# One decoder layer on one core: modulation sums moved off the spatial gating unit, the mLSTM's first ends four ticks later, the last k tiles taken result by result

## The chip, the cores and the metric

The kernel runs on one core of a Trainium2 chip. The metric is the device time of one execution in microseconds (us). Engines are named as the profile names them: PE is the matrix engine, PEld its weight load, DVE the vector engine, ACT the scalar engine, POOL is GpSimd, and SP issues all DMAs of this kernel. "L1045" is line 1045 of the kernel before.

## The reference, cut to what matters

One layer is applied to x (2048 tokens x 1024 channels, float32). From the vector c come six modulation vectors; two parallel branches and an attention are computed from one projection:

```python
mod = silu(c) @ w_ada + b_ada            # 6 x 1024: shift, scale, gate, twice
h = rms_norm(x, g_mix) * (1 + sc1) + sh1
p = h @ w_in                             # q,k,v of attention; q,k,v,o and gates of mLSTM; u,v of the spatial unit
y = concat(forgetting_attention(...), sigmoid(o_m) * rms_norm(mlstm_chunkwise(...)),
           spatial_gating(gelu(u_s), gelu(v_s)))
x = x + gt1 * (y @ w_out)
h = rms_norm(x, g_ffn) * (1 + sc2) + sh2
x = x + gt2 * conv_ffn(h, w_up, w_conv, b_conv, w_down)
```

The mLSTM ends with h / max(|den|, exp(-m)) and an RMS norm over the 64 channels of each head. Every large product is computed from float32 split in two parts, with three matmuls for one (`mm3`, L53 to L56: high*high, high*low, low*high).

## The kernel before, in words

**Stages.** The kernel runs the projection of x into p (about the first 710 us of the profile), attention, the output projection, the up-projection with convolution, and the down-projection. Only the projection and the very end of the down-projection are touched.

**Steps and blocks.** The projection goes over two halves of the tokens (1024 each) and, in each half, over seven column blocks of w_in. That makes 14 steps, numbered n = 0 to 13: in the first half 0 km (mLSTM's k with the gates, 272 columns), 1 qo (mLSTM's q and o, 512), 2 vm (mLSTM's v, 256), 3 sgu (the spatial unit's u and v, 512), 4 k, 5 q, 6 v of the attention (512 each); in the second half 7 to 13 in the same order. A step has eight blocks, i = 0 to 7. A block is 24 matmuls into one PSUM tile `acc` (three buffers in turn) and then its consumer: `use_km`, `do_qo`, `use_vm`, `use_sgu`, `use_qk`, `use_v`.

**Ticks.** Everything else is threaded between the matmuls by hand, by `tick` (L627). `products` (L601) calls it at the end of each block and, where the block is 512 columns wide, also in its middle, after the fourth of eight k. This text writes "4-5m" for the middle tick of block 5 of step 4, and "4-5e" for its end. One tick does three things in this order: `due()` runs what was put off by `after(n, f)`, n ticks ago; then, in a middle tick, one segment of `chores`; then one segment of the first generator in `background`.

- `chores` holds `rest_of_mod` (L449): 64 modulation sums (L466, L468: one DVE instruction each over a 128x512 tile of w_ada) in eight groups of eight. Each segment also issues the next tile's DMA (L458). When a group ends, `columns_or_row` (L478) is put off by two ticks: it multiplies the group's sum by ones on PE (L488 for shift and scale, L482 for a gate) into the PSUM tile `mp`, which has one buffer, and DVE (L491, L493) or ACT (L484) reads it from there.
- `background` holds, one after another, `rows` (gates of the mLSTM) and `mlstm(qi)` (L925), qi = 0 to 3, one per 512 tokens. `mlstm` has 21 segments, one per tick: segments 1 to 3 issue loads and wait; 4, 5, 9 and 12 call `turned`, which transposes k into the same tile `mp` (L963) for ACT to copy (L965); 6 to 16 work through four chunks; 17 is the start of the end (L1028 to L1042: the division L1034, the output gate's load L1036, the square L1038, its sum L1040, the power on POOL L1042); 19 multiplies (L1045, `hq`); 21 transposes `hq` on PE (L1052) and writes the result (L1054, L1055). mlstm(0) and mlstm(2) begin in steps 2 and 9 at block 4, so that their segments 5 to 20 lie in the sgu steps 3 and 10 and segment 21 in 4-0m and 11-0m; mlstm(1) and mlstm(3) follow directly and end in 5-2e and 12-2e.

**Who orders the work.** In steps 1 to 5 and 8 to 12 the written order holds on every engine (`tc.manual_schedule`). In steps 0, 6, 7 and 13, and in all later stages, a planner orders the instructions of each engine by their place in the text and by when it reckons that their inputs are ready. Each engine runs its instructions in order, and so does SP with the DMAs.

**The end.** The down-projection (`Down`, L1431) makes each product p from 11 k tiles; `prep` splits a tile's operands into four halves (tag `wsp`, 12 buffers, three tiles' worth) three steps ahead of `mm` (L1494), which for every k adds to four results `db` in turn. After the last product (p = 3 of the second half) `last(i)` multiplies each result by the gate (L1568), adds the rest (L1569) and writes it out (L1570).

Of the kernel before, what the change touches and what calls it, by code (L numbers as in the profile page):

```python
# [12 lines left out]
ALU = mybir.AluOpType  # L13
# [20 lines left out]
def trunk(  # L34
# [7 lines left out]
    V, A, G, T = nc.vector, nc.scalar, nc.gpsimd, nc.tensor  # L42
# [4 lines left out]
    def bc(ap, axis, n):  # L47
        u = ap.unsqueeze(axis)
        shape = list(u.shape)
        shape[axis] = n  # L50
        return u.broadcast_to(shape)

    def mm3(ps, lh, ll, rh, rl, start, stop, resume=False):  # L53
        T.matmul(ps, lh, rh, start=start, stop=False, skip_group_check=resume)  # L54
        T.matmul(ps, lh, rl, start=False, stop=False, skip_group_check=resume)  # L55
        T.matmul(ps, ll, rh, start=False, stop=stop, skip_group_check=resume)  # L56
# [104 lines left out]
    def load_v(h, cs):  # L161
        for c in cs:
            dma(
                kv[h][2][:, 4 * c : 4 * c + 4].bitcast(F32),
                v_d[c * TB : (c + 1) * TB, h, :].rearrange("(n p) d -> p n d", p=P),
            )
# [235 lines left out]
    def load_x(tt):  # L402
        xt = pool.tile([P, D], F32, name="xt", tag="t4k")
        dma(xt, x[tt * P : (tt + 1) * P, :])
        return xt
# [128 lines left out]
    def head_setup():  # L534
        rest_of_columns()
        dma(gsgu, g_sgu.broadcast_to([P, 256]))
        dma(gbias[:, 0:8], b_fox_f.broadcast_to([P, 8]))
        dma(gbias[:, 8:12], b_m_i.broadcast_to([P, 4]))
        dma(gbias[:, 12:16], b_m_f.broadcast_to([P, 4]))
        wsn = pool.tile([P, 4, P], F32, name="wsn", tag="sq")  # L540
        dma(wsn, w_s[0].rearrange("g t s -> t g s"))
        for g in range(4):
            G.affine_select(
                wsn[:, g, :], wsn[:, g, :], pattern=[[-1, P]], compare_op=ALU.is_ge, fill=0.0,
                base=0, channel_multiplier=1,
            )
        ps = misc_ps()
        for g in range(4):
            T.transpose(ps[:, g * P : (g + 1) * P], wsn[:, g, :], ident)
        A.copy(wT.rearrange("p g t -> p (g t)"), ps)  # L550
# [4 lines left out]
    def make_h(tb, xin=None):  # L555
        xs = xin if tb == 0 else norm_x(xin or [load_x(tb * 4 + i) for i in range(4)])
        for k in range(KT):
            ps = (tr_ps, acc_ps)[k % 2]() if tb == 0 else tr_ps()
            for i in range(4):
                T.transpose(ps[:, i * P : (i + 1) * P], xs[i][:, k * P : (k + 1) * P], ident)  # L560
            h32 = pool.tile([P, TB], F32, name="h32", tag="t2k")
            hh = pool.tile([P, TB], F32R, name="hh", tag="hT")
            hl = pool.tile([P, TB], F32R, name="hl", tag="hT")
            A.activation(h32, ps, AF.Identity, bias=sh1[:, k : k + 1], scale=a1[:, k : k + 1])
            V.tensor_copy(hh, h32)
            V.tensor_tensor(hl, h32, hh.bitcast(F32), op=ALU.subtract)  # L566
            hT[tb, k] = (hh, hl)
# [54 lines left out]
    pending = []  # L622
    chores, started = [], []
    background = []
    ticks = [0]

    def tick(middle=False):  # L627
        ticks[0] += 1
        due()
        if middle and chores and started and next(chores[0], True):  # L630
            chores.pop(0)
        if background and next(background[0], True):
            background.pop(0)
# [19 lines left out]
    def due(everything=False):  # L653
        for item in pending[:]:
            if everything or item[0] <= ticks[0]:
                pending.remove(item)
                item[1]()
# [267 lines left out]
    def mlstm(qi):  # L925
# [5 lines left out]
        got = {}  # L931
# [46 lines left out]
        for n in range(4):  # L978
# [44 lines left out]
            if n < 3:  # L1023
                decay(n + 1)
                yield

        den = pool.tile([P, 4, 4], F32, name="den", tag="den")
        nd = pool.tile([P, 4, 4], F32, name="nd", tag="nd")  # L1028
        V.tensor_scalar(nd, H[:, :, :, 64], -1.0, None, op0=ALU.mult)
# [3 lines left out]
        hn = H[:, :, :, 0:64]  # L1033
# [2 lines left out]
        dma(om, om_d[:, :, t0 : t0 + 512].rearrange("j p t -> p j t"))  # L1036
        hq = pool.tile([P, 4, 4, 64], F32, name="hq", tag="t4k")
        A.activation(hq, hn, AF.Square)  # L1038
        ss = pool.tile([P, 4, 4], F32, name="mss", tag="mss")
        V.tensor_reduce(ss, hq, axis=AX.X, op=ALU.add)  # L1040
        V.tensor_scalar(ss, ss, 1.0 / 64, EPS, op0=ALU.mult, op1=ALU.add)
        G.tensor_tensor(ss, ss, nhalf[:, 0:1].unsqueeze(2).broadcast_to([P, 4, 4]), op=ALU.pow)  # L1042
        yield
        yield
        V.tensor_tensor(hq, hn, bc(ss, 3, 64), op=ALU.mult)  # L1045
        hq2 = hq.rearrange("p n h d -> p n (h d)")
        yield
        yield
# [28 lines left out]
    for n, (half, i) in enumerate(steps):  # L1077
        if i == 0:
            make_h(half * 2, x0)
            if half == 0:  # L1080
                head_setup()
            make_h(half * 2 + 1)
        elif n == nb - 1:
            x0 = [load_x(8 + t) for t in range(4)]
        if n == len(steps) - 1:
            while background:
                if next(background[0], True):
                    background.pop(0)
            n_accs[0] = 2
            pool.close("proj_r")  # L1090
            pp.close("proj_r")
            attention_open_right()

            load_k(0)
            first_rows = [], []
            first = [scores(0, tb, load_q(0, tb, "qA"), r) for tb, r in zip((1, 0), first_rows)]
            load_v(0, (0, 1))
            background += first
        nxt[0] = Weights(blocks[steps[n + 1][1]][0]) if n + 1 < len(steps) else None
        if i == 1:  # L1100
            written.enter_context(tc.manual_schedule())
        blocks[i][1](half, cur)
        started.append(n)
        if nxt[0]:
            nxt[0].cast()
        cur = nxt[0]
        if n in (nb - 2, 2 * nb - 2):
            written.close()
        if i == 0:
            log_gates(half)  # L1110
            background += [rows(half * 2), rows(half * 2 + 1)]
        if i == 2:
            background.append(mlstm(half * 2 + 1))
        if n == nb + 2:
            small_setup()
# [312 lines left out]
    KH = 11  # L1428
    n_bank = [0]

    class Down:  # L1431
# [62 lines left out]
        def mm(self, p, k):  # L1494
            more = p == 3
            if k == 0:
                if more:
                    self.ps[3] = self.ps[5]
                else:
                    n_bank[0] += 1  # L1500
                    tag = "db%d" % ((n_bank[0] - 1) % 2)
                    self.ps[p] = [pp.tile([P, 512], F32, name="db", tag=tag) for _ in range(4)]
            ah, al, bh, bl = self.sl.pop((p, k))
            for i in range(4):
                sl = slice(i * P, (i + 1) * P)
                mm3(self.ps[p][i], ah[:, sl], al[:, sl], bh, bl, not more and k == 0, k == KH - 1, resume=more)

        def rest(self, ti, nl, i):

# [236 lines left out]
```

## Time and profile before

| | |
|---|---|
| three timed runs | 2603.63, 2607.26, 2610.91 us; median 2607.26 us |
| the profiled execution | 2607.8 us, of which the span from first to last instruction is 2606.1 us |
| granted PE clock | 0.997 |
| DVE, ACT, POOL busy | 2010.0, 1272.8, 402.5 us |

In the answers of the trace a row of the timeline gives start (us from the span's start), duration, engine, line, operation, output <- inputs and shapes, and in brackets the time that the engine was idle before it and what ended that. "x4" merges four instructions. Waits are listed as "who <- for whom: total us, times, longest". PE's matmuls overlap: the shown end of one lies after the start of the next, so a matmul's duration is not its pace.

### The profile page before, as it was taken

What the parts mean: (1) busy time and instruction counts of PE and PEld (TensorE: products, weight loads), DVE (VectorE), ACT (ScalarE), POOL (GpSimd) and SP (SyncE); (2) the same over time, 40 slices, a digit from 0 to 9 for tenths busy, and PEclk for the clock granted to TensorE, in tenths of its full rate; (3) what the DMA queues carried; (4) which work ended last, traced back from release to release, by engine and by line L of the source; (5) the groups of instructions that cost most, each with busy time, mean ns of one, the idle gap of its engine ahead of it and who ended that gap; (6) DMA issues with size and microseconds to landing.
All of it is one profiled execution on the core that took longest, in us unless ns stands there. A gap on an engine that the chain in (4) does not pass through costs nothing.

```text
span 2606.1 us, 36311 instructions
## 1 busy us (share of the span) xinstructions
PE 2530.5 (97%) x12521; PEld 2097.9 (81%) x12537; DVE 2010.0 (77%) x3438; ACT 1272.8 (49%) x2424; POOL 402.5 (15%) x532
## 2 busy tenths in 40 slices
PE   5999999999999999999989999999999999999999
PEld 5888888888787877777868888888888888888787
DVE  7657666476388889866589888888888887997797
ACT  4333343432388878844455544454444444444443
POOL 2012310132266556520000000000000000000000
PEclk9999999999999999999999999999999999999999
DMA  7345763454664445266632222255222217658523
GB/s 247 107 120 160 209 209 88 129 152 138 180 164 123 129 126 166 58 195 224 248 89 92 79 89 82 81 201 187 90 81 81 90 65 279 210 176 290 184 93 117
DMA packets 302592, 379.58 MB, mean 146 GB/s; under 512 B 31934, under 2 KB 194588, under 8 KB 300360
## 3 DMA queue, kind: packets, MB, share of 16 engines
q1 hardware_dynamic: 302408, 377.26, 46.1%
q8 instruction: 99, 1.62, 0.3%
q14 instruction: 85, 0.70, 0.1%
HBM read 276.44 MB, written 100.74 MB: 145 GB/s over the span
## 4 chain that ended last, share of the span: by engine, by line
PE 81%; DVE 9%; DMA 4%; ACT 3%; issue 2%; POOL 1%; SPq 0%; DVEq 0%; ACTq 0%; POOLq 0%
PE ub L56 11%; PE ub L54 11%; PE ub L55 11%; PE acc L54 6%; PE acc L56 6%; PE acc L55 6%; PE db L55 4%; PE db L56 4%; PE db L54 4%; PE sp L206 3%; PE tp L259 3%; PE op L245 2%; PE op L246 2%; PE wps L55 2%; PE wps L54 2%
## 5 line engine op out<-in xcount | busy, mean ns | idle before, releaser
L54 PE MATMUL acc<-wh,hh 128*128 128x512 f32 (+2 forms) x768 | 285.5, 373 | 1.9 <-DVE vhl L762 1.2
L54 PE MATMUL ub<-T,wsph 128*128 128x512 f32 x704 | 274.2, 390 | 5.8 <-ACT wsph L1358 5.8
L56 PE MATMUL ub<-T,wspl 128*128 128x512 f32 x704 | 273.7, 389 | 1.6 <-DVE wspl L1359 1.6
L56 PE MATMUL acc<-wh,hl 128*128 128x512 f32 (+2 forms) x768 | 274.2, 360 | 0.3 <-DVE hl L566 0.3
L55 PE MATMUL acc<-wl,hh 128*128 128x512 f32 (+2 forms) x768 | 273.9, 358 | 0.2
L55 PE MATMUL ub<-T,wsph 128*128 128x512 f32 x704 | 273.9, 389 | 0.0
L55 PE MATMUL db<-wspl,wsph 128*128 128x512 f32 x616 | 240.6, 391 | 3.6 <-DVE wspl L1490 3.5
L56 PE MATMUL db<-wsph,wspl 128*128 128x512 f32 x616 | 239.6, 389 | 0.0
L54 PE MATMUL db<-wsph 128*128 128x512 f32 x616 | 238.3, 389 | 0.3 <-ACT wsph L1489 0.3
L1358 ACT CAST wsph<-S 128x512 fp32r<-128x512 f32 x176 | 109.7, 623 | 228.4 <-PE ub L55 162.8
L263 DVE TENSOR_TENSOR plo<-tp,phi 128x512 fp32r<-128x512 f32 (+1 forms) x320 | 187.0, 607 | 31.6 <-ACT phi L262 29.4
L54 PE MATMUL ub<-B,wsph 128*128 128x512 f32 x528 | 207.1, 392 | 2.8 <-ACT wsph L1358 2.8
L56 PE MATMUL ub<-B,wspl 128*128 128x512 f32 x528 | 207.2, 392 | 0.6 <-DVE wspl L1359 0.6
L55 PE MATMUL ub<-B,wsph 128*128 128x512 f32 x528 | 207.0, 392 | 0.0
L223 ACT ACTIVATE L<-L,nm 128x1024 f32<-128x1024 f32 (+2 forms) x192 | 172.6, 903 | 36.0 <-DVE nm L212 34.7
L262 ACT CAST phi<-tp 128x512 fp32r<-128x512 f32 (+1 forms) x320 | 160.0, 521 | 40.2 <-PE tp L259 38.9
L259 PE MATMUL tp<-ident,L 128*128 128x128 f32 x1088 | 177.0, 274 | 2.5 <-POOL L L228 0.6
L206 PE MATMUL sp<-kk,q 128*128 128x512 f32 (+3 forms) x640 | 169.2, 375 | 3.3 <-DVE nm L212 2.2
L1489 ACT CAST wsph<-act 128x512 fp32r<-128x512 f32 x132 | 82.3, 623 | 179.0 <-PE db L55 162.2
L228 POOL TENSOR_SCALAR L<-L,rs 128x1024 f32<-128x1024 f32 (+2 forms) x192 | 167.2, 881 | 11.0
L56 PEld LDWEIGHTS acc<-wh,hl 128*128 128x128 f32 x768 | 145.0, 190 | 22.3 <-DVE hl L566 0.8
L54 PEld LDWEIGHTS acc<-wh,hh 128*128 128x128 f32 x768 | 146.2, 191 | 20.7 <-DVE vhl L762 1.4
(333 smaller groups left out, 5942.9 us busy)
## 6 DMA issues: line engine op xcount, KB each, us to landing
w<-in_w_up_dram SPq DMA_DIRECT2D x88, 512.0 KB
wd<-in_w_down_dram SPq DMA_DIRECT2D x176, 256.0 KB
wa<-in_w_ada_dram SPq DMA_DIRECT2D x96, 256.0 KB
act_d<-yc SPq DMA_DIRECT2D x44, 512.0 KB
act<-act_d SPq DMA_DIRECT2D x44, 512.0 KB
wr<-in_w_in_dram SPq DMA_DIRECT2D x64, 256.0 KB
q<-q_d SPq DMA_DIRECT2D x128, 128.0 KB
hc_d<-hl SPq DMA_DIRECT2D x28, 512.0 KB
```

Of the source, the lines that this page charges most:

```text
L54: T.matmul(ps, lh, rh, start=start, stop=False, skip_group_check=resume)
L55: T.matmul(ps, lh, rl, start=False, stop=False, skip_group_check=resume)
L56: T.matmul(ps, ll, rh, start=False, stop=stop, skip_group_check=resume)
L206: T.matmul(sp[:, b : b + bw], q2[n][:, qs], kk[:, s0 + b : s0 + b + bw], start=n == 0, stop=n == 1 and not last)
L223: A.activation(L[c], L[c], AF.Exp, bias=nm[:, n - 1 : n], scale=-1.0, accum_out=rs[:, c : c + 1])
L228: G.tensor_scalar(t, t, rs[:, 0:1], 1.0, op0=ALU.mult, op1=ALU.mult)
L245: T.matmul(op[:, c0:], vv[:, j, :], hi[:, c0:], start=(j == 0), stop=False)
L259: T.transpose(tp[:, i * P : (i + 1) * P], rows[i][j // 8][:, (j % 8) * P : (j % 8 + 1) * P], ident)
L262: A.copy(hi[:, c0:], tp[:, c0:])
L263: V.tensor_tensor(lo[:, c0:], tp[:, c0:], hi[:, c0:].bitcast(F32), op=ALU.subtract)
L1358: A.copy(hi, src)
L1489: A.copy(hi, v)
```

## The change

Four edits.

1. A modulation sum is now run in a middle tick of any step but sgu (n % 7 == 3), and besides in every other tick of steps 2 and 9 (vm) and 7 (km), which have end ticks only. Steps 3 and 10 lose eight sums each; steps 2, 7 and 9 get four each, and step 12 has five where it had one.
2. mlstm(0) and mlstm(2) wait four ticks before their end. In all four, one tick more lies between the square (L1038) and its sum, and one more between the power and the product `hq`, which goes from DVE to POOL.
3. A loop that ran `background` dry ahead of step 13 is gone (an assertion stands for it).
4. In the very last product the matmuls of k = 8, 9 and 10 are held until k = 10 and then made result by result: nine for result 0, nine for result 1, and so on.

```diff
     def tick(middle=False):
         ticks[0] += 1
         due()
-        if middle and chores and started and next(chores[0], True):
+        block = started[-1] + 1 if started else 0
+        in_block[0] = in_block[0] + 1 if in_block[1] == block else 1
+        in_block[1] = block
+        if chores and (middle and block % 7 != 3 or block in (2, 7, 9) and in_block[0] % 2) and next(chores[0], True):
             chores.pop(0)
...
+        if qi % 2 == 0:
+            for _ in range(4):
+                yield
         den = pool.tile([P, 4, 4], F32, name="den", tag="den")
...
         A.activation(hq, hn, AF.Square)
+        yield
         ss = pool.tile([P, 4, 4], F32, name="mss", tag="mss")
...
         yield
         yield
-        V.tensor_tensor(hq, hn, bc(ss, 3, 64), op=ALU.mult)
+        yield
+        G.tensor_tensor(hq, hn, bc(ss, 3, 64), op=ALU.mult)
...
         if n == len(steps) - 1:
-            while background:
-                if next(background[0], True):
-                    background.pop(0)
             n_accs[0] = 2
...
+            assert not background and not chores
             background += first
...
-            ah, al, bh, bl = self.sl.pop((p, k))
+            ks = [k]
+            if more and self.H == 1 and k > KH - 4:
+                ks = range(KH - 3, KH) if k == KH - 1 else ()
+            got = [self.sl.pop((p, j)) for j in ks]
             for i in range(4):
                 sl = slice(i * P, (i + 1) * P)
-                mm3(self.ps[p][i], ah[:, sl], al[:, sl], bh, bl, not more and k == 0, k == KH - 1, resume=more)
+                for j, (ah, al, bh, bl) in zip(ks, got):
+                    mm3(self.ps[p][i], ah[:, sl], al[:, sl], bh, bl, not more and j == 0, j == KH - 1, resume=more)
```

More of the change, by code (lines that the diff above doesn't have):

```diff
@@ L624, in trunk @@
     background = []
-    ticks = [0]
+    ticks, in_block = [0], [0, 0]
     def tick(middle=False):
```

## The prediction

> **What bounds the kernel now.** First the page: the span and the busy shares.
>
> ```profile
> span 2606.1 us, 36311 instructions
> PE 2530.5 (97%) x12521; PEld 2097.9 (81%) x12537; DVE 2010.0 (77%) x3438; ACT 1272.8 (49%) x2424; POOL 402.5 (15%) x532
> ```
>
> PE is the bound over the whole span, and only 75.6 us of idle PE are left. The change takes no matmul away, so what it can win is idle PE time and the tail after the last matmul. Next, the waits of PE between 60 and 700 us, which is the projection:
>
> ```profile
> PE mps L1052 <- DVE hq L1045: 6.8, 4, 2.7
> PE trp L560 <- ACT h L564: 2.1, 1, 2.1
> PE acc L54 <- DVE vhl L762: 1.2, 1, 1.2
> PE trp L560 <- DVE xt L523: 1.0, 3, 0.5
> PE sp L206 <- DVE nm L212: 0.8, 2, 0.7
> ```
>
> Only the first group lies in the steps with a written order: the transposes at the mLSTM's end wait for `hq`, once for each of the four. The timeline of PE at the four:
>
> ```profile
> 211.45 0.39 PE L56 MATMUL acc<-wh,hl 128*128 128x512 f32 x1
> 214.53 1.06 PE L1052 MATMUL mps<-ident,hq 128*128 128x128 f32 x8 [2.69 <-DVE hq L1045]
> 215.36 0.48 PE L54 MATMUL acc<-wh,hh 128*128 128x512 f32 x1
> ...
> 294.55 0.60 PE L784 MATMUL trp<-ident,qn 128*128 128x128 f32 x4
> 296.03 1.09 PE L1052 MATMUL mps<-ident,hq 128*128 128x128 f32 x8 [0.88 <-DVE hq L1045]
> ...
> 545.89 1.06 PE L1052 MATMUL mps<-ident,hq 128*128 128x128 f32 x8 [2.69 <-DVE hq L1045]
> ...
> 625.86 0.60 PE L784 MATMUL trp<-ident,qn 128*128 128x128 f32 x4
> 626.96 1.09 PE L1052 MATMUL mps<-ident,hq 128*128 128x128 f32 x8 [0.49 <-DVE hq L1045]
> ```
>
> The bracket understates the loss, since the shown end of a matmul is later than the start of the next. The pace is read from starts, here in the last three k tiles of the run:
>
> ```profile
> 2591.65 0.39 PE L54 MATMUL db<-wsph 128*128 128x512 f32 x1
> ...
> 2593.24 0.39 PE L55 MATMUL db<-wspl,wsph 128*128 128x512 f32 x1
> ...
> 2599.58 0.39 PE L56 MATMUL db<-wsph,wspl 128*128 128x512 f32 x1
> ```
>
> These are the first, the eighth and the last of 36 matmuls: 7.93 us over 35 steps, 0.227 us each. So the transposes after 211.45 were due at 211.68 and came at 214.53: 2.85 us lost. The wait at 545.89 has the same bracket and counts the same. Eight transposes take 0.83 us to the next start (214.53 to 215.36), four 0.42; the other two lost 296.03 - 294.55 - 0.42 = 1.06 and 626.96 - 625.86 - 0.42 = 0.68. Together **7.4 us**.
>
> Why they wait, from DVE and POOL in step 3:
>
> ```profile
> 203.89 1.22 DVE L1034 TENSOR_TENSOR H<-H,den 128x1024 f32<-128x1024 f32 x1
> 207.80 3.27 POOL L1042 TENSOR_TENSOR mss<-mss,nhalf 128x16 f32<-128x16 f32 x1 [3.88 <-DVE mss L1041]
> 211.04 0.91 POOL L712 TENSOR_TENSOR ev<-ev 128x256 f32<-128x256 f32 x1
> 212.51 0.74 DVE L468 SCALAR_TENSOR_TENSOR modacc<-wa,cs,modacc 128x512 f32<-128x512 f32 x1
> 213.17 1.22 DVE L1045 TENSOR_TENSOR hq<-H,mss 128x1024 f32<-128x1024 f32 x1
> ```
>
> From the division to the end of `hq` pass 10.5 us (203.89 to 214.39). The power was done at 211.07, but DVE came to `hq` at 213.17, behind the spatial unit (whose next instruction waited for the POOL product of 211.04) and a modulation sum.
>
> **The change part by part.**
>
> *The first and third end.* The division moves to 4-0m, sum and power to 4-0e, `hq` to 4-2m, the transposes to 4-3m, and likewise in step 11. Rows that fall on these ticks:
>
> ```profile
> 220.92 0.95 PE L488 MATMUL mp<-ones,modacc 128*128 128x1 f32 x8
> 227.87 1.64 POOL L128 TENSOR_TENSOR ss<-ss,nhalf 128x8 f32<-128x8 f32 x1 [4.25 <-DVE ss L771]
> 228.18 1.02 PE L735 MATMUL trp<-sv,wT 128*128 128x256 f32 x4
> 235.91 0.60 PE L744 MATMUL trp<-ident,sy 128*128 128x128 f32 x4
> ```
>
> 4-0m is 214.53, 4-1m 220.92, 4-2m 228.18, 4-3m 235.91: 21 us for the chain that took 10.5. The product on POOL is not in the trace. Its nearest rows are the POOL products of 256 elements:
>
> ```profile
> L712 POOL TENSOR_TENSOR ev<-ev 128x256 f32<-128x256 f32 x16 | 11.0, 685 | 90.0 <-DVE ev L710 90.0
> ```
>
> Four times 0.685 is 2.7 us; the slow one of 211.04 (0.91) gives 3.6. I take 2.7, the mean of sixteen. POOL reaches it after the k block's power, at 227.87 + 1.64 = 229.5, so `hq` is ready at 232.2, at worst 233.1, ahead of 235.91. I count the whole 5.7 us of the two long waits. POOL's next power of the k block is at most 3.6 us late; the normalised k is transposed three ticks (some 10 us) after it is made, which covers that. If that cover went, PE would wait what is left of the 3.6 us. DVE loses 1.22 us of work for each end.
>
> *The second and fourth end* get six ticks in place of four. Two ticks are 7 us (220.92 to 228.18); they were 1.06 and 0.68 us late and the product becomes 1.5 us longer. I count 1.7 us.
>
> In both, the load of the output gate moves with the division. On SP it stood in the sgu step behind a buffer that the mixing still held; in the k step those are long free, so weights queued behind it come no later. Nothing counted.
>
> *The sums that move.* Each is 0.74 us of DVE and one 256 KB load on SP. The load by stage (columns after the length: busy PE, PEld, DVE, ACT, POOL, then PE's clock, DMA share, GB/s):
>
> ```profile
> 100.00:150.00 50.00, 49.93 (x323) 45.25 (x321) 26.49 (x52) 15.19 (x28) 0.61 (x1) 1.00 0.50 143
> 350.00:400.00 50.00, 46.91 (x287) 41.22 (x286) 29.10 (x66) 23.67 (x50) 1.65 (x3) 1.00 0.50 167
> ```
>
> Beside the vm steps DVE has half its time free: four sums, 3.0 us, cost nothing, and if a tile landed late, the three `acc` buffers cover two narrow blocks. In step 7 the order is the planner's, and the second half's input is being normalised on DVE for a PE that waits for it (the two L560 waits above). There four sums cost between nothing and 3.0 us. The planner puts later work into DVE's gaps first, so I take 0.3. The sums that left steps 3 and 10 gain nothing beyond the waits already counted, since PE waits for nothing else there. The loop taken out found nothing to run: mlstm(3) ended in 12-2e, and now ends in 12-6e, still ahead of step 13.
>
> *A wait that is added.* The second and the seventh group of sums now end in 4-4m and 11-4m, so `columns_or_row` runs in 4-5m and 11-5m. mlstm(1) and mlstm(3) now start in 3e of these steps, so their segment 4 falls into the same tick, right behind. Both write `mp`, a single buffer: the k transposes (L963), and all matmuls queued behind them on PE, wait until DVE or ACT has read it. The rows for how fast it is read, the first from the chain of work that ended last:
>
> ```profile
> 221.08 0.79 PE mp L488 x8
> ...
> 221.91 0.16 DVE L491 COPY sh<-mp 128x4 f32<-128x4 f32 x1
> ...
> 284.99 0.95 PE L488 MATMUL mp<-ones,modacc 128*128 128x1 f32 x8
> 289.19 0.15 DVE L493 SCALAR_TENSOR_TENSOR a<-mp,colA 128x4 f32<-128x4 f32 x1
> ...
> 552.73 0.80 PE L54 MATMUL acc<-wh,hh 128*128 128x512 f32 x1
> 553.33 0.57 ACT L484 COPY gr<-mp 1x512 f32<-1x512 f32 x1 [2.94 <-PE mp L482]
> ```
>
> For the shift (4-5m): L488 at 220.92 was read by 222.07; with 0.14 us from a DVE end to PE (214.39 to 214.53) PE would go on at 222.21 in place of 220.92 + 0.79 = 221.71, 0.5 us later. For the gate (11-5m): read by 553.90, PE on at 554.04 in place of about 553.1 (552.73 and two paces), 0.9 us later. Bounds: nothing, or the read of 289.19, 4.2 us behind its product, which makes 289.34 + 0.14 - 285.78 = 3.7 us. There DVE stood in the mLSTM's end; in 4-5m it doesn't, so I take the quick reads: **+1.4 us**.
>
> *The last product.* DVE at the end:
>
> ```profile
> 2592.89 0.69 DVE L1490 TENSOR_TENSOR wspl<-wd,wsph 128x512 fp32r<-128x512 f32 x1
> ...
> 2597.97 1.37 DVE L1568 TENSOR_TENSOR o<-db,gt 128x512 f32<-128x512 f32 x2 [4.39 <-PE db L56]
> ...
> 2601.66 1.28 DVE L1569 TENSOR_TENSOR o<-o,s 128x512 f32<-128x512 f32 x2
> ```
>
> Now results come three matmuls apart (0.68 us) and each needs two DVE instructions (1.28 us), so DVE is behind and ends at 2602.94. Held back, they come nine apart (2.04 us), and only the last is left at the end: it starts 0.43 us after its last matmul's start (2597.97 against 2597.54, nine paces before 2599.58), so 2600.01 + 1.28 = 2601.3, **1.6 us** earlier. Against that, the eighth matmul of the 36 is now one of k = 10 and needs the half that is ready at 2593.58; with the 0.14 PE gets it at 2593.72 in place of 2593.24: 0.5 us. Net **-1.1**, bounds 0 and -1.6.
>
> Sum: -7.4 + 0.3 + 1.4 - 1.1 = -6.8 us. The profiled execution took 2607.8 us, which is 0.5 above the median of the three runs: 2601.0 for such an execution, **2600.5 us** against the median of 2607.26.
>
> **The rivals.**
>
> *POOL and DVE hold each other up.* POOL's product of 256 took 0.61 to 0.91 us; where it was slow, DVE ran beside it. If the long product takes DVE's work with it, `hq` or the block's evictions come late. At 1.5 times its length the product still ends by 233.6, so this needs a delay of over 2.3 us more; at 2 us lost in each of two ends the time is 2604.5. The Trainium skill, SBUF — State Buffer, "Who interferes with whom", says that a DVE instruction with two SBUF inputs and a GpSimd instruction that reads SBUF exclude each other for a whole instruction; no run here shows it over 1024 elements.
>
> *The reads of `mp` come late* (3.7 us twice in place of 1.4 in all): 2606.5.
>
> *The other side: sums hold step 7.* If the planner sets the four sums ahead of the normalisation, each stops DVE, and so PE, for its 0.74 us and for the rest of its load. An input tile's load in this place held the chain thus:
>
> ```profile
> 379.87 3.75 DMA xt<-in_x_dram
> ```
>
> Sum and whole load are 4.5 us, four times 18: 2618. It decides against the change from 1.8 us a sum. For it speaks that DVE feeds PE there; against it, that each tile is loaded one sum ahead.
>
> *More is won*: `mp` read in time, no cost in step 7, the whole 1.6 us at the end, give -9.0, 2598.3. *It does not do what it says*: the four waits stay, and only the end is won, 2606.
>
> **How the numbers follow.** Forecast 0.58; more won 0.16; late reads 0.10; hold-up 0.06; waits stay 0.05; step 7 0.05. About 0.3%, 7.8 us, is what a measurement of this kernel can tell from no change: the three runs lie 7.3 us apart. 2599.4 is 0.3% faster, and the forecast is 1.1 us short of it, less than medians of three move. So a quarter of the forecast's chance and nearly all of "more won" count as faster: 0.30. Slower by over 0.3% (2615.1) is the heavier part of step 7: 0.04. Same: 0.66. The range runs from 2596, below "more won" by that spread, to 2607.5, which takes in late reads and the kept waits and leaves out step 7.
>
> **What would show it.** The L1052 waits are gone from PE's waits; new waits of L963 at 4-5m and 11-5m, 0.3 to 1 us; `hq` on POOL at 2.7 us; one DVE pair after the last matmul; PE in 300 to 400 us busy as before. A wait of L1052 for POOL, an L560 wait longer than 2.1 us, or other waits in the planned stages would make me wrong.

## The result, and the profile after

The changed kernel took 2614.44 us (median of 13 runs, 2608.68 to 2616.07) against 2606.47 us (13 runs, 2602.38 to 2610.91): ratio 1.0026, 95% interval 1.0018 to 1.0035. It is slower by some 7 us, where 2600.5 was forecast, and 2614.44 lies outside the range of 2596 to 2607.5. The profiled execution took 2615.29 us, 7.5 more than that of before (2607.8).

The head of the page after (busy us, share of the span, instructions):

```profile
span 2613.5 us, 36336 instructions
PE 2533.8 (97%) x12537; PEld 2097.7 (80%) x12537; DVE 2010.7 (77%) x3434; ACT 1272.4 (49%) x2424; POOL 406.2 (16%) x536
```

DVE, ACT and POOL do the same work as before within 4 us, and PE's share is the same. The waits of PE between 60 and 700 us (who <- for whom: total us, times, longest). Lines moved: L1060 is the transposes that were L1052, L738 the mixing (L735), L966 the k transposes (L963), L1006 the mLSTM's second product (L1003):

```profile
PE acc L54 <- ACT wh L595: 3.2, 1, 3.2
PE trp L738 <- DVE sy L739: 1.9, 4, 0.8
...
PE mps L1006 <- DVE sc L992: 1.5, 2, 0.8
PE mp L488 <- DVE modacc L474: 1.3, 1, 1.3
PE mp L482 <- DVE modacc L474: 1.3, 1, 1.3
...
PE mp L966 <- ACT kT L968: 1.2, 1, 1.2
...
PE acc L55 <- DVE wl L596: 0.7, 1, 0.7
PE mp L966 <- ACT gr L484: 0.7, 1, 0.7
...
PE mp L966 <- DVE sh L491: 0.3, 1, 0.3
```

The 6.8 us of waits at the transposes are gone, as forecast, and these nine groups stand there that before did not have (a tenth, 0.4 us, is in step 7). That the loss is made in the projection shows in the last eviction of its last block, on ACT, first before, then after:

```profile
711.61 0.37 ACT L761 CAST vhl<-acc 128x256 fp32r<-128x256 f32 x1 [0.49 <-DVE vhl L762]
```

```profile
722.31 0.37 ACT L764 CAST vhl<-acc 128x256 fp32r<-128x256 f32 x1 [0.49 <-DVE vhl L765]
```

After is 10.7 us late there and 7.4 us late at its end (the two spans). Part of the difference is the tail of the last product (below); 1.9 us are made up somewhere in the later stages, which I did not follow.

**The costliest new wait** is at the start of step 6. PE's timeline after:

```profile
331.01 0.40 PE L56 MATMUL acc<-wh,hl 128*128 128x512 f32 x1
334.58 0.80 PE L54 MATMUL acc<-wh,hh 128*128 128x512 f32 x1 [3.17 <-ACT wh L595]
336.08 0.79 PE L55 MATMUL acc<-wl,hh 128*128 128x512 f32 x1 [0.71 <-DVE wl L596]
...
338.81 0.63 PE L56 MATMUL acc<-wh,hl 128*128 128x512 f32 x1
339.24 0.63 PE L54 MATMUL acc<-wh,hh 128*128 128x512 f32 x1
...
340.50 0.39 PE L54 MATMUL acc<-wh,hh 128*128 128x512 f32 x1
```

The bracket says 3.17 us, but the matmuls behind it start 0.43 us apart (338.81 to 339.24) in place of 0.23, until 340.50. From the matmul before the wait, at 331.01, to 340.50 PE started ten matmuls and four transposes: 10 x 0.227 + 0.42 = 2.7 us of work in 9.5, so 6.8 us are lost: 4.6 in the two waits (3.57 and 1.50 us from start to start, where 0.227 each was due), the other 2.2 to the slower pace. What came late, from DVE, SP and ACT after:

```profile
317.84 0.68 DVE L596 TENSOR_TENSOR wl<-wr,wh 128x512 fp32r<-128x512 f32 x1
...
324.26 1.40 DVE L1062 SCALAR_TENSOR_TENSOR yt<-mps,colA,om 128x512 f32<-128x512 f32 x2
...
326.36 1.90 DVE L596 TENSOR_TENSOR wl<-wr,wh 128x512 fp32r<-128x512 f32 x3
```

```profile
324.63 0.44 SPq L404 DMA_DIRECT2D xt<-in_x_dram  x1
...
327.08 0.93 SPq L585 DMA_DIRECT2D wr<-in_w_in_dram  x1
```

```profile
333.91 0.62 ACT L595 CAST wh<-wr 128x512 fp32r<-128x512 f32 x1 [4.85 <-DMA wr<-in_w_in_dram]
```

and the casts, the load and the cast that needs it in the kernel before:

```profile
315.66 0.68 DVE L596 TENSOR_TENSOR wl<-wr,wh 128x512 fp32r<-128x512 f32 x1
...
323.50 1.90 DVE L596 TENSOR_TENSOR wl<-wr,wh 128x512 fp32r<-128x512 f32 x3
```

```profile
324.22 0.35 SPq L585 DMA_DIRECT2D wr<-in_w_in_dram  x1
```

```profile
327.85 0.62 ACT L595 CAST wh<-wr 128x512 fp32r<-128x512 f32 x1
```

The end of mlstm(1) now stands among the casts of step 6's weights. The casts come 2.9 us later (326.36 against 323.50), so the raw weights' buffer comes free later and the next load is issued 2.9 us later (327.08 against 324.22). Of the 2.9 us, 2.2 are there two casts earlier (317.84 against 315.66): the end's power holds POOL for 3.27 us from 310.90, so the q block's own power and with it `qn` on DVE come 1.4 us later (315.80 against 314.39), and the sum behind `qn`, beside POOL's product, takes 1.51 us where the one that stood there took 0.74. The end's products L1062, right ahead of the casts, add the last 0.7. From issue to cast the load then takes 6.8 us where it took 3.6 at most, and the cast runs 6.1 us later (333.91 against 327.85). It goes out behind an input tile of 512 KB (324.63; the last of these went out at 307.55 before) and two stores of `yt` (325.71); that these slow it is likely, but no run took them away. The load was the last of its step, so nothing was left to hide it.

### The profile page after: what moved, and what is told of

Read it like the earlier page. It is cut to its first block, busy times and chain, and to the rows that moved or that the text cites. A ratio compares the mean times of both kernels' runs of the same rounds, so it can differ in the third digit from the quotient of the medians.

```text
span 2613.5 us, 36336 instructions
## 1 busy us (share of the span) xinstructions
PE 2533.8 (97%) x12537; PEld 2097.7 (80%) x12537; DVE 2010.7 (77%) x3434; ACT 1272.4 (49%) x2424; POOL 406.2 (16%) x536
## 4 chain that ended last, share of the span: by engine, by line
PE 44%; DVE 5%; DMA 1%; issue 1%; ACT 0%; SPq 0%; DVEq 0%; ACTq 0%
PE ub L56 11%; PE ub L54 10%; PE ub L55 10%; PE db L55 4%; PE db L56 4%; PE db L54 4%; DVE wspl L1496 2%; DMA wd<-in_w_down_dram 1%; PE wps L54 0%; PE wps L56 0%; PE wps L55 0%; DVE T L1191 0%; DMA s<-x_d 0%; DVE t2w L1476 0%; DVE t2w L1481 0%
## 5 line engine op out<-in xcount | busy, mean ns | idle before, releaser
L55 PE MATMUL acc<-wl,hh 128*128 128x512 f32 (+2 forms) x768 | 274.9, 360 | 0.9 <-DVE wl L596 0.7
L55 PE MATMUL ub<-T,wsph 128*128 128x512 f32 x704 | 273.9, 389 | 0.0
L55 PE MATMUL db<-wspl,wsph 128*128 128x512 f32 x616 | 240.2, 390 | 2.6 <-DVE wspl L1496 2.5
L55 PE MATMUL ub<-B,wsph 128*128 128x512 f32 x528 | 206.9, 392 | 0.0
L228 POOL TENSOR_SCALAR L<-L,rs 128x1024 f32<-128x1024 f32 (+2 forms) x192 | 167.3, 882 | 11.0
```

The lines of the kernel that those rows point to most:

```text
L228: G.tensor_scalar(t, t, rs[:, 0:1], 1.0, op0=ALU.mult, op1=ALU.mult)
```

## The experiments

Each ratio is against runs of before on the same chip, with its 95% interval; it stands as recorded and is not the quotient of the two medians. My first theory was that the moved ends cost the time, by putting their work ahead of other work in the engines' order; the rival, that the moved sums do. The next questions were what in the ends costs, and whether they can be moved without it.

| kernel | median us | before | ratio |
|---|---|---|---|
| tail_only | 2607.59 | 2608.0 | 1.0001 (0.9992 to 1.0009) |
| sums_only | 2608.33 | 2608.0 | 1.0002 (0.9994 to 1.0011) |
| ends_only | 2613.66 | 2608.0 | 1.0023 (1.0013 to 1.0033) |
| no_four | 2618.96 | 2608.0 | 1.0043 (1.0030 to 1.0055) |
| late_turn | 2610.03 | 2607.03 | 1.0006 (0.9997 to 1.0015) |
| late_turn_tail | 2608.85 | 2607.03 | 1.0006 (0.9997 to 1.0015) |
| cols_late | 2615.53 | 2607.03 | 1.0034 (1.0021 to 1.0047) |
| xt_early | 2614.49 | 2607.03 | 1.0025 (1.0016 to 1.0034) |
| split | 2620.37 | 2608.21 | 1.0052 (1.0039 to 1.0066) |
| split_tail | 2614.35 | 2608.21 | 1.0026 (1.0017 to 1.0036) |
| sums_late | 2608.88 | 2608.21 | 1.0009 (1.0000 to 1.0017) |
| split2 | 2612.62 | 2607.65 | 1.0015 (1.0005 to 1.0024) |
| **split2_tail** | 2604.88 | 2607.65 | **0.9987 (0.9978 to 0.9996)** |
| split2_shift | 2615.84 | 2606.98 | 1.0032 (1.0020 to 1.0045) |
| **split3_tail** | 2603.80 | 2606.98 | **0.9986 (0.9978 to 0.9995)** |

### One edit at a time

**tail_only** is before with edit 4 alone, **sums_only** with edit 1 alone, **ends_only** with edit 2 alone (the hunks are those of the change). **no_four** is the whole change without

```diff
-        if qi % 2 == 0:
-            for _ in range(4):
-                yield
```

> The kernel before with edit 4 alone (the last product result by result). Both theories say the same: 1.1 us less than before (between 0 and 1.6), the last DVE instruction pair 1.3 us after the last matmul instead of two pairs behind, and one PE wait of about 0.5 us at the eighth matmul of the last 36.

> The kernel before with edit 1 alone (where the modulation sums run). Theory 'order' (the moved ends of the mLSTM stand on DVE and ACT ahead of work that PE needs soon; the sums by themselves do no harm): the two long L1052 waits shrink from 2.85 us by one or two sums of 0.74 us each, no wait at the start of step 6, no wait of L482 or L488 for the sum, so 1.5 to 3 us less than before. Rival 'sums' (the moved sums are what costs, through their loads, DVE time and the single mp buffer): the waits of L966 for mp, of L482 and L488 for the sum and the 3 us wait for the last weight tile at the start of step 6 are here too, 5 us or more above before.

> The kernel before with edit 2 alone (the mLSTM's ends later, hq on POOL). Theory 'order': the four L1052 waits (7.4 us) are gone, but the waits of the mixing (L735 for sy, 2.6 us in two steps), of L1003 for sc (1.9 us), for the last weight tile at the start of step 6 (5.3 us with the slower clock behind it) and for kT (1.4 us) come; 2 to 5 us above before. Rival 'sums': without the moved sums none of them comes, and the time is 5 to 7 us below before.

> The changed kernel without the four ticks for mLSTM 0 and 2 (their ends stay in the sgu step with six ticks from division to transposes, and mLSTM 1 and 3 end in 5-4e and 12-4e). Theory 'order': the mixing waits (2.6 us), the wait for the last weight tile (5.3 us) and the waits for the group sum (2.9 us) go, L1060 waits under 0.5 us each: 5 to 8 us below before. Rival 'sums': the waits at mp, for the group sum and for the weight tile stay, since no sum is moved against the changed kernel: 3 us or more above before.

Edits 1 and 4 alone change nothing that can be measured; edit 2 alone brings 6 us of loss, nearly as much as all four (1.0023 against 1.0026). So the loss lies with the ends, and the sums by themselves are not its cause. They are not free either: in sums_only PE's waits at the transposes fall from 6.8 to 5.4 us, and 1.6 us of waits for `kT` (L966) come, so a gain and a loss cancel. The four ticks are not the culprit either: without them it is 4.5 us worse (2618.96 against 2614.44), with waits for weight casts at the start of steps 4, 6 and 11, at L55 (5.4 us in PE's waits between 60 and 700 us), and waits of the transposes for POOL's `hq` (2.1 us). Here my theory 'order' missed: the waits at `mp` (2.2 us) and for the groups' sums (1.5 us each) stayed, as the rival said.

### Is the wait at the transposes worth what it shows?

**late_turn** moves the four transposes one tick later and nothing else (so the wait has time to pass); **late_turn_tail** is the same with edit 4.

```diff
         V.tensor_tensor(hq, hn, bc(ss, 3, 64), op=ALU.mult)
         hq2 = hq.rearrange("p n h d -> p n (h d)")
         yield
         yield
+        yield
```

> The kernel before with one extra tick between the product hq (still on DVE) and its transposes on PE, in all four mLSTM ends; nothing else is moved on DVE, ACT or POOL within an end. Theory 'order' (what costs is the moved DVE and ACT work, not the waiting transposes): the four L1052 waits are at most 2.85 us late against a tick of 3.5 us or more, so they go, and nothing else comes: 6 to 7.4 us below before. Rival 'clock and chance' (a wait removed in one place returns elsewhere in the in-order queues whatever is moved): within 2 us of before.

> The kernel of late_turn with edit 4 (last product result by result) besides. Theory 'order': 7 to 8.5 us below before, that is about 1 us below late_turn, too little to tell the two apart with certainty. Rival: within 2 us of before.

The wait at the transposes is gone in both, and the time is no better than before. PE in late_turn, at the first end:

```profile
214.29 0.50 PE L55 MATMUL acc<-wl,hh 128*128 128x512 f32 x1 [1.63 <-DVE wl L596]
...
216.22 0.80 PE L55 MATMUL acc<-wl,hh 128*128 128x512 f32 x1 [0.96 <-DVE wl L596]
...
220.23 0.63 PE L54 MATMUL acc<-wh,hh 128*128 128x512 f32 x1
220.65 0.63 PE L55 MATMUL acc<-wl,hh 128*128 128x512 f32 x1
```

and DVE there:

```profile
212.41 1.22 DVE L1045 TENSOR_TENSOR hq<-H,mss 128x1024 f32<-128x1024 f32 x1
213.55 0.68 DVE L596 TENSOR_TENSOR wl<-wr,wh 128x512 fp32r<-128x512 f32 x1
...
215.48 0.68 DVE L596 TENSOR_TENSOR wl<-wr,wh 128x512 fp32r<-128x512 f32 x1
```

The next thing that PE needs, the last weight casts of step 4, stands on DVE behind `hq` and behind the spatial unit. PE stops 2 us later for those, twice, and then goes at 0.42 us a matmul for a while. From 212.27 to 222.34 PE starts fourteen matmuls and eight transposes, 4.0 us of work in 10.1, so 6.0 us are lost at this end, where before lost 2.85. The wait at the transposes had covered this: DVE was late there for everything, not for `hq` alone. It is the point that the prediction missed when it asked what is late next.

**sums_late** is late_turn with edit 1, which takes eight sums of 0.74 us off DVE in each sgu step.

> Before with edit 1 and with the transposes of the mLSTM's end one tick later. If the modulation sums are the backlog that holds the weight casts at the start of steps 4 and 11, each cast comes 0.7 us and more earlier than in late_turn and the 5.2 us of waits at L55 fall to 3 or less: 2604 to 2607 us. If the last casts wait for the spatial unit's round trips between DVE and POOL, they stay where they were, the waits of 5 us stay, and the time is 2608 to 2611 us.

The waits at L55 fell from 5.2 to 3.0 us, so part of the backlog is the sums; but waits for edit 1's own sums came up instead (L488 and L482 for `modacc`, 1.3 us each, and a cast, 1.1), and the time stayed at that of before, above what the first theory gave.

### Single waits of the changed kernel

**cols_late** puts off `columns_or_row` by four ticks in place of two, so that it no longer meets mlstm's k transposes in `mp`; **xt_early** issues three of the four loads of the second half's input one step earlier, at the start of step 5, further from the weights of step 6.

```diff
-                after(2, lambda acc=acc, col=col: columns_or_row(acc, col))
+                after(4, lambda acc=acc, col=col: columns_or_row(acc, col))
```

```diff
+        elif n == nb - 2:
+            x0 = [load_x(8 + t) for t in range(3)]
         elif n == nb - 1:
-            x0 = [load_x(8 + t) for t in range(4)]
+            x0.append(load_x(11))
```

> The changed kernel with the groups' sums multiplied four ticks after they end in place of two (columns_or_row moves from 5m to 6m). Theory 'order': the waits of L966 for mp (0.46 and 0.86 us) and of L488 and L482 for the group sum (1.46 and 1.45 us) go, the rest stays: about 4 us below the changed kernel, so 2 to 4 us above before. Rival 'sums': these are the main loss, and the time falls to before or below.

> The changed kernel with three of the four input tiles of the second half loaded at the start of step 5, where the buffers are free, in place of together behind the output gate's load late in step 5. If the bunched input loads delay the last weight tile of step 6, the PE wait of L54 for L595 at the start of step 6 falls from 3.2 us to 1 us or less, the granted clock from 330 to 340 us stays at 1.0, and the time is 4 to 5 us below the changed kernel. If instead DVE frees the weight buffer late (the result products L1062 ahead of the casts), the wait stays at 2.5 us or more and the time within 1.5 us of the changed kernel.

Neither wins time. In cols_late the waits of L966 for `sh` and `gr`, of L1006 and of L488 and L482 are all gone, but L966 now waits 3.4 us for `kT` at 492 us and the other waits stay. In xt_early the wait for the cast at the start of step 6 falls from 3.2 to 1.4 us, and the time is that of after. But the cast comes no earlier there (334.66 against 333.91): PE comes to it later (it starts the matmul before the wait at 333.54, against 331.01), in part since seven matmuls from 312.65 went at half pace. Nor did the run clear the way for that load: in after three of the four input tiles go out at 302.65, and the fourth, the one just ahead of the weights, still is in xt_early (325.57). So it decides nothing on what slows the load. In cols_late taking some waits away lets PE run into others: as in late_turn, DVE and ACT are behind, not one tile. A fifth buffer for the raw weights, which would let that load start earlier, was not tried.

### The ends without the shift

In after the first end takes six ticks more, and since `background` runs one generator at a time, mlstm(1) and mlstm(3) come six ticks later as a whole. **split** keeps the moved ends but runs them as a thread of their own, so that the next mLSTM begins when it did before (its tile `H` is taken only where it is first written); **split_tail** is the same without edit 1.

```diff
+        if ends and next(ends[0], True):
+            ends.pop(0)
         if background and next(background[0], True):
             background.pop(0)
...
-        if qi % 2 == 0:
-            for _ in range(4):
-                yield
+        end = wind_up(qi, t0, ecol, H)
+        if qi % 2 == 0:
+            ends.append(end)
+            for _ in range(4):
+                yield
+        else:
+            yield from end
...
+    def wind_up(qi, t0, ecol, H):
+        if qi % 2 == 0:
+            for _ in range(3):
+                yield
```

> The kernel after, but the moved ends of the first and third mLSTM run as a thread of their own, beside the start of the second and fourth, which begin at the tick at which they began before the change. Theory 'shift': what costs is that everything of the second and fourth mLSTM comes six ticks later and lands on other work. Then the waits at L482 and L488 for modacc (1.5 us each), at L966 (0.5 and 0.9 us), at L1006 (1.0 us twice) and the 5.3 us at the start of step 6 go, the 1.3 us beside the mixing in steps 4 and 11 stay, and the time is some 4 us below before: 2600 to 2605 us where before is 2607. Rival 'load': the ends are too much for DVE wherever they stand in steps 4 and 11; then the same or other waits of 5 us and more stand in steps 4 to 6 and the time stays within 2 us of after.

> As split, but with the modulation sums where they were before the change (edits 2 and 4 alone). 'Shift' gives the same 2600 to 2605 us, without the wait of 1.2 us at the start of step 10 (L966 for kT), since steps 2 and 9 carry no sums. If the sums beside the spatial unit are what keeps DVE behind, waits for weight casts (L54, L55) of 2 us and more come back at the start of steps 4 and 11 and it is 3 us and more slower than split.

Both expectations for the time were wrong, though the waits went as 'shift' said: in split those of L1006, at step 6 and, but for 0.4 us, those of the k transposes (L967 there) are gone. Those for the groups' sums (L488 and L482, 1.4 us each) stay, though they were to go. A new one took their place, which I had not seen coming:

```profile
237.73 1.89 PE L991 MATMUL mps<-qz,kT 128*128 128x256 f32 x4 [3.96 <-DVE yt L1073]
```

The end's transposes now fall into the tick of the next mLSTM's first products, and both want the two `mps` buffers: some 4.15 us lost by starts, in each half. **split2** and **split2_tail** (split and split_tail, with the two ticks inside the first and third end left out) move the transposes to 4-2m and 11-2m, where only one of those buffers is in use:

```diff
         A.activation(hq, hn, AF.Square)
-        yield
+        if qi % 2:
+            yield
...
         yield
         yield
-        yield
+        if qi % 2:
+            yield
         G.tensor_tensor(hq, hn, bc(ss, 3, 64), op=ALU.mult)
```

> As split, but in the first and third end the two added ticks inside the chain are left out, so its transposes come at 4-2m and 11-2m in place of 4-3m and 11-3m, where the second and fourth mLSTM take both mps buffers for their first products. Theory 'shift': the two waits of 4.15 us at L991 for yt go and nothing takes their place, so the time falls by 8 us against split, to 2610 to 2613 us; what is left above before is the two waits of the sums' last addition (1.6 us each), the mixing (1.3 us twice) and stretches of lower clock. Rival 'load': other waits of 3 us and more in steps 4 and 11.

> split2 with the modulation sums where they were before the change (edits 2 and 4 alone). 'Shift': the 8.3 us of split_tail's waits at mps go, and of before's 7.4 us some 3 are left as other waits: 2602 to 2606 us where before is 2607 to 2608. 'Load': no better than 2608.

split2_tail is faster than before, the only question being by how much: 0.04 to 0.22%. These are the waits of split2_tail between 60 and 700 us that before has not, but for one of 0.5 us in step 7:

```profile
PE trp L737 <- DVE sy L738: 3.3, 4, 1.5
...
PE acc L55 <- DVE wl L596: 0.7, 1, 0.7
```

and of split2, which differs by edit 1:

```profile
PE trp L740 <- DVE sy L741: 4.2, 4, 1.9
PE mp L967 <- ACT kT L969: 2.3, 2, 1.6
...
PE mp L488 <- DVE modacc L474: 1.5, 1, 1.5
PE mp L482 <- DVE modacc L474: 1.5, 1, 1.5
```

So the sums, which cost nothing by themselves, cost 7.7 us here (2612.62 against 2604.88, one chip): 0.9 + 2.3 + 3.0 - 0.7 = 5.5 us of it is in these rows. Where PE stood still for the ends anyway (sums_only), DVE had time to make the sums good; where it no longer does, they show.

**split2_shift** adds to split2_tail the late start alone; **split3_tail** makes the sum of squares of the first and third end one tick later.

```diff
             ends.append(end)
-            for _ in range(4):
+            for _ in range(10):
                 yield
```

```diff
         A.activation(hq, hn, AF.Square)
-        if qi % 2:
-            yield
+        yield
...
         yield
-        yield
         if qi % 2:
             yield
+            yield
         G.tensor_tensor(hq, hn, bc(ss, 3, 64), op=ALU.mult)
```

> split2_tail with one thing added: the second and the fourth mLSTM begin six ticks later, as in after; the ends stand where they stand in split2_tail, and the sums where they stood before. Theory 'shift': the waits at L1003 for sc (about 1 us in each half) and the 5 us at the start of step 6 (L54 for the cast wh, L55 for wl) come back, and it is 6 to 9 us slower than split2_tail, 2610 to 2614 us. Rival: if only the two ticks inside the ends, or the ends beside those mLSTMs, made the difference, it stays within 2 us of split2_tail.

> split2_tail with the sum of squares of the first and third end one tick later (4-0e, 11-0e), so that POOL's power over 16 columns comes behind the k block's power and no longer ahead of it; product and transposes stay. If DVE's wait for that power is what holds the mixing in split2_tail (1.65 us at L737, twice), this falls below 1 us and the time by 1 to 3 us, to 2602 to 2604; against it, the product may come too late for the transposes at 4-2m, a wait of 1 to 3 us at L1069, twice, and then it is no faster than split2_tail.

The shift alone costs 11.0 us (2615.84 against 2604.88; by the ratios, 0.0045 x 2607 = 11.7), more than the 6 to 9 expected. The waits that it brings back in split2_shift are those of after:

```profile
PE acc L54 <- ACT wh L595: 2.8, 2, 2.5
PE acc L55 <- DVE wl L596: 2.4, 4, 1.1
...
PE mps L1005 <- DVE sc L991: 1.5, 2, 0.8
```

They sum to 6.7 us, 6.0 more than in split2_tail. The clock behind them is slower (0.75 in the stretch of 330 to 340 us, 0.91 in the next ten, 0.67 from 690 to 700), which may be the rest; the profiled execution of split2_shift was the slowest of its six and that of split2_tail the fastest of its twelve, so the two traces differ by more (20.0 us) than the kernels do. In split3_tail POOL's power over 16 columns still came ahead of the k block's, so it does not answer what it was built for; its time is that of split2_tail, and it too is faster than before.

## Why the prediction was wrong, point by point

The terms by starts, from the profiled execution of after; a loss that both kernels have is left out.

| step of the prediction | forecast us | measured us |
|---|---|---|
| the four waits at the transposes go | -7.4 | -7.5 |
| `mp`: k transposes behind `columns_or_row` | +1.4 | +1.3 |
| sums in step 7 | +0.3 | +0.1 |
| sums in the vm steps | 0 | +1.8 |
| groups of sums that end in steps 5 and 12 | 0 | +2.9 |
| the end's work in 4-0 and 11-0, beside the mixing | 0 | +2.6 |
| mlstm(1), mlstm(3) six ticks later: L1006 | 0 | +1.9 |
| the same: start of step 6 | 0 | +6.8 |
| slower matmuls after 692 us | 0 | +1.4 |
| last product | -1.1 | -1.4 |

All but the last line add up to +11.3 us, against the 10.7 by which the last eviction of the projection is late. The 1.4 us after 692 us is luck as far as the runs show: behind the same four waits matmuls go at half pace in after, sums_only and late_turn, and at full pace in before, ends_only, split2 and split2_tail.

**Right: the four waits go, and their length.** `hq` came in time, and no L1060 wait is left. Only the product's length was off, to the safe side: 1.91 us where 2.7 was taken.

```profile
227.66 1.91 POOL L1053 TENSOR_TENSOR hq<-H,mss 128x1024 f32<-128x1024 f32 x1
```

**Right: the reads of `mp`**, forecast at 0.5 and 0.9 us; by starts they cost 0.46 and 0.86:

```profile
246.09 0.44 PE L966 MATMUL mp<-ident,kn 128*128 128x128 f32 x2 [0.26 <-DVE sh L491]
...
586.32 0.44 PE L966 MATMUL mp<-ident,kn 128*128 128x128 f32 x2 [0.67 <-ACT gr L484]
```

**Right: step 7 and the end.** The waits in 370 to 400 us sum to 3.6 us in both kernels. At the end one pair of DVE instructions is left after the last matmul:

```profile
2609.05 0.69 DVE L1578 TENSOR_TENSOR o<-db,gt 128x512 f32<-128x512 f32 x1 [0.62 <-PE db L56]
2609.78 0.69 DVE L1579 TENSOR_TENSOR o<-o,s 128x512 f32<-128x512 f32 x1
```

That ends 1.84 us after the last matmul's start (2608.63), where before it was 3.36: 1.5 us won, and the 36 matmuls lost only 0.1 of the 0.5 that was set against it. Such an amount is below what tail_only's runs can tell (-2.1 to +2.3 us).

**Wrong, and the step that failed: "The first and third end".** It followed the chain of the end itself and POOL behind it. It knew that mlstm(1) and mlstm(3) begin six ticks later, but of all the work that this pushes back it priced the meeting in `mp` alone (+1.4) and put the rest at nothing. `background` runs one generator after another, so whole mLSTMs move, with their DVE, ACT and POOL work, onto other work, the casts of step 6's weights above all: 8.7 us in the table (1.9 and 6.8), and 11 us in split2_shift, which adds that move to split2_tail.

The same step held that POOL's delay is covered, since the normalised k is transposed three ticks after it is made. PE did not wait for k. But DVE works in order: in 4-0e the end's power stands on POOL ahead of the k block's (2.90 us from 217.59), DVE waits 3.81 us for the latter at `qn`, and behind `qn` stands the mixing's `sy`, for which PE waits (2.6 us in the table). The sentence "DVE loses 1.22 us of work for each end" looked at DVE's sum; what counts is what stands ahead of a weight cast, or of `sy`, in DVE's order.

**Wrong: "I count the whole 5.7 us of the two long waits."** The wait was PE time that could be read off the trace, but not PE time to be had for nothing: late_turn removes it with one tick, and the casts behind are late instead. What is late next was asked of the end's own engines, not of PE.

**Wrong: "four sums, 3.0 us, cost nothing".** In the vm steps the price is not on DVE but in the loads. In step 9 ACT waits for weights, whose loads stand among those of the sums, and the copy that PE waits for is behind that cast:

```profile
490.28 0.62 ACT L595 CAST wh<-wr 128x512 fp32r<-128x512 f32 x1 [1.74 <-DMA wr<-in_w_in_dram]
490.80 0.36 ACT L968 COPY kT<-mp 128x256 f32<-128x256 f32 x1
```

In sums_only, which has edit 1 alone, PE waits for `kT` here too (1.1 us). That the load of the sum is what delayed the weights was not tried by itself. And the two groups that now end in step 5 and 12 put an addition ahead of a PE instruction that waits for it; DVE comes to it only after the group's last sum (308.02):

```profile
308.80 0.68 DVE L474 TENSOR_TENSOR modacc<-modacc,brow 1x512 f32<-1x512 f32 x1
```

```profile
309.53 1.05 PE L488 MATMUL mp<-ones,modacc 128*128 128x1 f32 x8 [1.30 <-DVE modacc L474]
```

In sums_only the addition comes at the same place (309.06), and PE, which there lost 1.9 us to `hq` at 294 us, comes to L488 at 310.09 and waits for nothing.

**The rivals.** The one on the other side (sums hold step 7, 2618) was the wrong mechanism: step 7 costs 0.1 us. *POOL and DVE hold each other up* was seen, and at step 6 above it is part of the delay of the casts. Here the sum beside POOL's long product took 1.78 us in place of 0.74, and ends 0.55 us after POOL's product does (230.12 against 229.57):

```profile
227.73 0.69 DVE L779 TENSOR_TENSOR qn<-acc,ss 128x512 f32<-128x512 f32 x1
228.34 1.78 DVE L468 SCALAR_TENSOR_TENSOR modacc<-wa,cs,modacc 128x512 f32<-128x512 f32 x1
```

The Trainium skill, SBUF — State Buffer, "Who interferes with whom", has it that a DVE instruction with two SBUF inputs and a GpSimd instruction that reads SBUF keep each other out. The rows agree: `qn`, with one input in PSUM, kept its 0.69 us beside the same product, and the sum, with two in SBUF, did not.

**What stays open.** Why the loss of the shift is 11 us where its waits show 6; how the 6.8 us at step 6 divide between the late casts and the slow load; and where in the later stages 1.9 us come back. The slower clock goes with the waits in most of these runs, but no kernel here took the clock apart from the waits.

## What to carry to other kernels

A wait on the bounding engine is worth its length only if what that engine needs next is ready: before pricing it, list for the next ten microseconds each tile that it will ask for and when the in-order engine ahead of it makes that tile. When a step of a threaded schedule is put off, everything behind it in the same thread moves too; price the whole thread, or give the step a thread of its own and look for the buffers that the two then share. Try the parts of a change together as well as alone: here the sums cost nothing beside a stall and 7.7 us without it.

## What the runs showed of the hardware

**The matrix engine's pace can fall by half after waits well below 3 us.** In late_turn, after two waits of 1.63 and 0.96 us with three matmuls between (at 214.29, 214.62 and 214.86), matmuls start 0.42 us apart (220.23 to 220.65) in place of 0.23; the single wait of 2.69 us in before is followed by no slow matmul. At the end of the projection both kernels have the same four waits (0.3, 0.8, 0.3 and 1.4 us by starts); after them before goes on at full pace and after does not. In the same way the wait at L488 is followed by no slow matmul in after (1.30 us, to 309.53), and in xt_early (1.31 us, to 310.47) by seven that start 0.43 us apart from 312.65 on. The windows (columns as in the prediction: the clock is the third number from the end), first before, where these waits fall into 680 to 690 us, then after:

```profile
680.00:690.00 10.00, 8.61 (x39) 6.69 (x40) 3.95 (x13) 4.75 (x15) 7.50 (x13) 1.00 0.58 184
```

```profile
330.00:340.00 10.00, 6.12 (x19) 4.32 (x18) 5.05 (x13) 5.45 (x16) 2.76 (x3) 0.68 0.80 248
...
690.00:700.00 10.00, 8.60 (x33) 6.62 (x32) 2.85 (x10) 3.86 (x14) 6.82 (x12) 0.83 0.58 184
```

The Trainium skill, TensorE: Matmul & The Clock Gate, Part 1, describes a free-running window of about 3.4 us after which an idle engine is clocked at half rate. The halved pace agrees, and a window that runs freely would make the same waits cost in one execution and not in another; that a whole window must be idle is not borne out here, since the four waits at 690 us sum to 2.8 us with work between them, and the wait at 310.47 in xt_early is 1.31 us. A wait can so cost more than its length: to the 4.6 us of the two waits at step 6 the slow pace added 2.2, and in late_turn it added 3.1 to 2.9.

**POOL's time is not in proportion to the elements.** The 128x1024 product took 1.91 us, against 0.69 for 128x256 (the mean of L712, another product: 2.8 times for four times the elements) and 1.22 on DVE. One and the same POOL instruction, the scaling at L228, shows it by itself: in the mean it took 0.40 us for 128x128, 0.69 for 128x512 and 1.13 for 128x1024 (the profile of after), 2.8 times the time for eight times the elements.
